# The query latents of a hybrid attention layer, projected beside the first norm, one tile ahead

## The chip, the cores and the metric

The kernel runs on one core of one Trainium2 chip. The metric is the device time of one execution in microseconds (us), as the median of several runs. A profiled execution of the same program gives the trace; its times count from the start of its span. In the text PE is TensorE (PEld its weight loads), DVE is VectorE, ACT is ScalarE, POOL is GpSimd, and SP is the engine that issues the DMAs here.

## The reference

One layer of a streaming encoder on x of 1024 frames by 1024 channels, all in float32. What matters here is the start:

```
h   = rms_norm(x, ln_mix_pre)
z   = h @ w_in                      # 1024 x 5824 columns
qa, ka, va, cq, ckv, k_rope, g_a, g_b = split(z)   # 1024,1024,1024,384,256,64,1024,1024
...                                 # differential attention from rope(qa), rope(ka), va
cq  = rms_norm(cq, q_a_norm)        # the query latents
qb  = cq @ w_uq                     # later: the second attention (latent, 8 heads)
...
merged = sigmoid(g_a) * y_a + sigmoid(g_b) * y_b
x   = x + rms_norm(merged @ w_o, ln_mix_post)
x   = x + rms_norm(SwiGLU(rms_norm(x, ln_ffn_pre)), ln_ffn_post)
```

Only cq's place in the program changes; nothing that is computed does.

## The kernel before, in words

Every float32 matrix product is made of three matmuls on two-part operands (a high and a low part, `mm3`, lines 266 to 269: high by high on L267, high by low on L268, low by high on L269). So each operand must first be split: ACT writes the high part, and DVE or POOL subtracts to get the low part (`split_sbuf`, lines L254 and L256, for loaded weights; `split_psum`, L260 and L261, for results in PSUM).

The start of the program (the prologue) works on tiles of 128 frames, from tile 7 down to tile 0. `norm_x` (L422 on) loads a tile of x, squares and sums it on ACT (L439), makes 1/rms with a small DVE step (L245) and a power on POOL (L247), scales it on DVE (L441), transposes it on PE in two groups of four (L447), and splits each group into hT, which all projections read. `da_proj` (L546) loads the weights of one head of the differential attention, splits them, and projects tile after tile with 24 matmuls of 384 columns each; then it applies the rotary tables (`rope`), which `rotary_tables` computes on DVE in the prologue. In the main program (L1335 on) head 0 of `da_proj` runs beside `norm_x`.

Then the eight heads of the differential attention follow. Beside the attention of each head (`interleave`) the PE is given filler work: the next head's projection and what the table `FILL` (L63) names: numbers are gate tiles (`gate_tile`, 48 matmuls of 512 columns each), "cq" and "ckv" are the latents (`latents`, L482). "cq" is done beside head 2: per tile of frames 24 matmuls of 384 columns, a square and sum on ACT (L500), 1/rms (L245, L247), a scaling on DVE (L502), three transposes on PE (L518) one tile later, a copy on ACT (L521) and a store. After the attention come the second attention, the merge (`mix_out`) and the feed-forward part, which the change doesn't touch in the source.

The program is written as one stream, from which a scheduler makes one fixed order per engine. Each engine takes its own instructions strictly in that order; an instruction waits at the head of its engine until the semaphores it names are reached. SBUF is dealt out by hand in zones (`Zone`), PSUM in banks (`Banks`). `cos_blk` and `sin_blk` are the rotary tables' two blocks.

## Time and profile before

| | |
|---|---|
| median of 3 runs | 2030.16 us (2027.11 to 2030.21) |
| profiled execution | 2029.12 us |
| its span, first to last instruction | 2027.1 us |
| PE busy in the span | 1968.2 us (97%) |
| DVE, ACT, POOL busy | 1162.7, 863.4, 537.7 us |
| PE waits in total, of that before its first instruction | 58.9 us, 11.8 us |
| granted PE clock, mean | 0.993 |

How to read it: PE is the engine that all others serve, so the time is PE's own work plus what it waits, plus what it loses while its clock is at the lower level. The total of the waits is the span less the busy time. The other engines are busy for little more than half of the span; what counts of them is only whether they deliver in time.

### The profile page before, as it was taken

How to read it: one execution, taken by the hardware profiler on the slowest of the kernel's cores; microseconds unless marked ns; L12 is line 12 of the kernel's file. 1: busy time of each engine (PE TensorE's matmuls, PEld its weight loads, DVE VectorE, ACT ScalarE, POOL GpSimd, SP SyncE). 2: the span in 40 equal slices, each digit the busy share in tenths (PEclk: the TensorE clock that was granted, in tenths of full speed). 3: DMA queues.
4: the chain of work that ended last, by engine and by line, in shares of the span. 5: the costliest groups of instructions: out<-in, count | busy, mean ns of one | idle time of the engine just before them, and what ended most of it. 6: DMA issues, size and time to landing. Idle time of an engine off the chain costs nothing. (4 is left out here: it accounts for less than half of the span.)

```text
span 2027.1 us, 28588 instructions
## 1 busy us (share of the span) xinstructions
PE 1968.2 (97%) x10400; PEld 1697.3 (84%) x10400; DVE 1162.7 (57%) x2464; ACT 863.4 (43%) x1912; POOL 537.7 (27%) x652
## 2 busy tenths in 40 slices
PE   6999999999999999999999998979999999999998
PEld 6898999989898988888978886757888888888886
DVE  7756757776775677786762355575344444343335
ACT  5435444554544446666663333343333323341102
POOL 2000010200000012222121212356554554452214
PEclk9999999999999999999999999989999999999999
DMA  5212111111212131450043533213222222262214
GB/s 169 69 47 81 44 57 51 56 49 43 77 33 77 35 111 53 132 174 29 32 149 100 168 125 107 91 63 94 76 90 84 73 94 73 102 231 83 83 32 145
DMA packets 148492, 176.49 MB, mean 87 GB/s; under 512 B 13536, under 2 KB 117376, under 8 KB 148352
## 3 DMA queue, kind: packets, MB, share of 16 engines
q1 hardware_dynamic: 148352, 174.68, 27.5%
q8 instruction: 81, 1.33, 0.3%
q14 instruction: 59, 0.48, 0.1%
HBM read 130.54 MB, written 44.11 MB: 86 GB/s over the span
## 5 line engine op out<-in xcount | busy, mean ns | idle before, releaser
L267 PE MATMUL PS<-AR 128*128 128x512 f32 (+3 forms) x2216 | 794.6, 361 | 4.7 <-ACT AR L254 2.0
L268 PE MATMUL PS<-AR 128*128 128x512 f32 (+3 forms) x2216 | 784.2, 355 | 3.7 <-POOL AR L256 3.7
L269 PE MATMUL PS<-AR 128*128 128x512 f32 (+3 forms) x2216 | 785.3, 356 | 1.7 <-POOL AR L256 1.7
L254 ACT CAST AR<-AFm 128x512 fp32r<-128x512 f32 (+4 forms) x514 | 301.3, 610 | 510.0 <-PE PS L1226 207.9
L267 PEld LDWEIGHTS PS<-AR 128*128 128x128 f32 x2216 | 417.2, 189 | 58.8 <-ACT AR L260 5.2
L268 PEld LDWEIGHTS PS<-AR 128*128 128x128 f32 x2216 | 418.7, 189 | 47.6 <-POOL AR L256 4.5
L269 PEld LDWEIGHTS PS<-AR 128*128 128x128 f32 x2216 | 417.4, 189 | 46.0 <-POOL AR L256 2.5
L256 POOL TENSOR_TENSOR AR<-AFm,AR 128x512 fp32r<-128x512 f32 (+4 forms) x203 | 310.0, 1533 | 459.8 <-ACT AR L254 408.6
L1226 PE MATMUL PS<-AR 128*128 128x512 f32 x1848 | 424.2, 391 | 5.4 <-POOL AR L256 3.7
L1226 PEld LDWEIGHTS PS<-AR 128*128 128x128 f32 x1848 | 348.0, 189 | 81.2 <-POOL AR L256 4.7
L256 DVE TENSOR_TENSOR AR<-AFm,AR 128x512 fp32r<-128x512 f32 (+5 forms) x311 | 212.7, 713 | 108.1 <-ACT AR L254 81.5
L260 ACT CAST AR<-PS 128x512 fp32r<-128x512 f32 (+3 forms) x320 | 135.2, 439 | 154.5 <-DVE AFm L388 70.6
L1235 DVE TENSOR_TENSOR AFm<-AFm,PS 128x512 f32<-128x512 f32 x110 | 75.3, 685 | 181.0 <-PE PS L1226 180.1
L261 DVE TENSOR_TENSOR AR<-PS,AR 128x512 fp32r<-128x512 f32 (+3 forms) x320 | 153.5, 497 | 40.1 <-ACT AR L260 38.1
L628 POOL CAST AR<-AR 128x128 fp32r<-128x128 f32 (+1 forms) x128 | 41.9, 327 | 455.4 <-PE PS L699 260.0
L658 ACT ACTIVATE AFm<-PS,nm 128x1024 f32<-128x1024 f32 (+3 forms) x192 | 142.7, 745 | 42.7 <-DVE nm L657 30.3
L657 DVE TENSOR_REDUCE nm<-PS 128x1 f32<-128x1024 f32 (+3 forms) x192 | 143.6, 752 | 3.3
L1298 DVE TENSOR_TENSOR AFm<-AFm,PS 128x512 f32<-128x512 f32 x80 | 54.4, 685 | 103.2 <-PE PS L269 103.2
L1190 DVE TENSOR_TENSOR AFm<-AFm 128x512 f32<-128x512 f32 x66 | 71.3, 1080 | 64.6 <-DMA s_aa<-AFm 27.6
L636 POOL MEMSET AR<- 128x256 f32 x64 | 21.2, 332 | 294.9 <-PE PS L269 244.8
L618 PE MATMUL PS<-idf,AFm 128*128 128x128 f32 x576 | 89.1, 275 | 2.5 <-ACT AR L260 0.6
L716 PE MATMUL PS<-AR 128*128 128x512 f32 (+5 forms) x384 | 87.1, 353 | 0.2 <-ACT AFm L658 0.2
(133 smaller groups left out, 1532.6 us busy)
## 6 DMA issues: line engine op xcount, KB each, us to landing
AFm<-in_w_in_dram SPq DMA_DIRECT2D x72, 192.0 KB
AFm<-in_w_ffn_gate_dram SPq DMA_DIRECT2D x22, 512.0 KB
AFm<-in_w_ffn_up_dram SPq DMA_DIRECT2D x22, 512.0 KB
s_aa<-AFm SPq DMA_DIRECT2D x44, 256.0 KB
AFm<-in_w_ffn_down_dram SPq DMA_DIRECT2D x22, 512.0 KB
AFm<-s_aa SPq DMA_DIRECT2D x22, 512.0 KB
AFm<-in_x_dram SPq DMA_DIRECT2D x16, 512.0 KB
AFm<-in_w_in_dram SPq DMA_DIRECT2D x32, 256.0 KB
```

What stands on the lines that cost most here:

```text
L254: nc.scalar.copy(h, src)
L256: e.tensor_tensor(out=l, in0=src, in1=f32v(h), op=ALU.subtract)
L260: nc.scalar.copy(h, src)
L261: nc.vector.tensor_tensor(out=l, in0=src, in1=f32v(h), op=ALU.subtract)
L267: nc.tensor.matmul(o, lhsT=sh, rhs=mh, start=first, stop=False)
L268: nc.tensor.matmul(o, lhsT=sh, rhs=ml, start=False, stop=False)
L269: nc.tensor.matmul(o, lhsT=sl, rhs=mh, start=False, stop=last)
L618: nc.tensor.transpose(tb.ap[:, q * P:(q + 1) * P], C[:, (g + q) * P:(g + q + 1) * P], idf)
L657: nc.vector.tensor_reduce(out=nm[:, m:m + 1], in_=src, axis=ax, op=ALU.max, negate=True)
L658: nc.scalar.activation(out=dst, in_=src, func=ACTF.Exp, bias=nm[:, m:m + 1], scale=1.0, accum_out=ss[:, m:m + 1])
L716: nc.tensor.matmul(sb.ap[:, c * 512:c * 512 + step], lhsT=qs.ap[:, m * 256 + v * P:m * 256 + v * P + P], rhs=kT[:, m, c * step:(c + 1) * s ...
L1226: nc.tensor.matmul(o, lhsT=v[:, ws, k], rhs=m, start=first and k == 0 and x == 0, stop=k == 3 and x == 2, skip_group_check=True)
```

## The change

The query latents cq leave the filler work beside head 2 and are projected in the prologue, tile by tile, right behind each tile's transposes. Their weights go to SBUF columns from 32768 on, which the attention uses later, so that the weights of `da_proj` can be loaded into their own zone while these are still in use. `norm_x` is cut in two: `scale(t)` (load, square, 1/rms, scaling) is now issued one tile ahead of the transposes, and it scales in place; the squares' unneeded output goes to `cos_blk`, and ln_mix_pre sits in `sin_blk`, so the rotary tables are written only behind the last scaling. `rotary_tables` starts with the third tile, as does `da_proj` of head 0. The gate tiles are dealt anew over the eight heads, 3, 2, 2, 0, 2, 2, 2, 3 (before 4, 2, 0, 0, 2, 2, 3, 3).

```diff
--- before.py
+++ after.py
@@ -60,7 +60,7 @@
 
 W_ENG = "dve"
 L_ENG = lambda nc: nc.vector
-FILL = ((0, 1, 2, 3), (4, 5), ("cq",), ("ckv",), (6, 7), (8, 9), (10, 11, 12), (13, 14, 15))
+FILL = ((0, 1, 2), (3, 4), (5, 6), ("ckv",), (7, 8), (9, 10), (11, 12), (13, 14, 15))
 PRE = 1
 DA_DEPTH = 1
 MLA_DEPTH = 2
@@ -426,20 +426,24 @@
             xts[t] = f_gen.alloc(D)
             nc.sync.dma_start(xts[t].ap, x2d[t * P:(t + 1) * P, :])
 
+        def scale(t):
+            ss = st("ss")
+            nc.scalar.activation(out=cos_blk.ap, in_=xts[t].ap, func=ACTF.Square, accum_out=ss)
+            r = rstd(ss, 1, D)
+            nc.vector.scalar_tensor_tensor(out=xts[t].ap, in0=xts[t].ap, scalar=r, in1=sin_blk.ap, op0=ALU.mult, op1=ALU.mult)
+
+
         load(NT - 1)
+        nc.sync.dma_start(sin_blk.ap, ln_mix_pre[0].partition_broadcast(P))
+        load(NT - 2)
+        scale(NT - 1)
         yield 0.0
-        wb = f_gen.alloc(D)
-        nc.sync.dma_start(wb.ap, ln_mix_pre[0].partition_broadcast(P))
         for t in reversed(range(NT)):
+            if t > 1:
+                load(t - 2)
             if t:
-                load(t - 1)
-            xt = xts.pop(t)
-            xs = f_gen.alloc(D)
-            ss = st("ss")
-            nc.scalar.activation(out=xs.ap, in_=xt.ap, func=ACTF.Square, accum_out=ss)
-            r = rstd(ss, 1, D)
-            nc.vector.scalar_tensor_tensor(out=xs.ap, in0=xt.ap, scalar=r, in1=wb.ap, op0=ALU.mult, op1=ALU.mult)
-            xt.free()
+                scale(t - 1)
+            xs = xts.pop(t)
             for g in range(2):
                 pb = ps_a.alloc()
                 for i in range(4):
@@ -451,15 +455,14 @@
                 pb.free()
             xs.free()
             yield 0.0
-        wb.free()
-
-
-    def load_win(lo, n, per):
+
+
+    def load_win(lo, n, per, zone=None):
 
         ws = []
         for k in range(0, NK, per):
             src = w_in[k * P:(k + per) * P, lo:lo + n].rearrange("(k p) c -> p k c", p=P)
-            ws.append(load_hl(src, f_raw, z_w, per * n, "p (k c) -> p k c", eng=W_ENG, k=per))
+            ws.append(load_hl(src, f_raw, zone or z_w, per * n, "p (k c) -> p k c", eng=W_ENG, k=per))
         return [(ws[k // per].h[:, k % per, :], ws[k // per].l[:, k % per, :]) for k in range(NK)], ws
 
     def gate_tile(j):
@@ -479,19 +482,20 @@
         for o in own:
             o.free()
 
-    def latents(which):
+    def latents(which, banks=ps_p, zone=None):
         if which == "cq":
             lo, n, nw, nrm, dst = 3072, 384, 384, q_a_norm, s_cq
         else:
             lo, n, nw, nrm, dst = 3456, 320, 256, kv_a_norm, s_ckv
-        w, own = load_win(lo, n, 1)
+        w, own = load_win(lo, n, 1, zone)
         wb = f_gen.alloc(nw)
         nc.sync.dma_start(wb.ap, nrm[0].partition_broadcast(P))
         nb = nw // P
         late = None
+        yield 0.0
         for t in reversed(range(NT)):
             sl = slice(t * P, (t + 1) * P)
-            pb = ps_p.alloc()
+            pb = banks.alloc()
             o = pb.ap[:, 0:n]
             for k in range(NK):
                 mm3(o, hT[:, k, 0, sl], hT[:, k, 1, sl], w[k][0], w[k][1], k == 0, k == NK - 1)
@@ -1335,18 +1339,21 @@
     all_slots = [[None] * 4 for _ in range(NH + 1)]
     nx, tab = norm_x(), rotary_tables()
     next(nx)
-    next(tab)
-    next(nx)
-    first = da_proj(0, all_slots[0], Banks(mp, 0, 6))
+    first, second = latents("cq", Banks(mp, 0, 6), Zone(mr, (32768, AR_COLS))), da_proj(0, all_slots[0], Banks(mp, 0, 6))
     next(first)
-    for _ in range(NT):
-        next(tab, None)
-        next(nx, None)
-        next(tab, None)
+    for t in range(NT):
+        next(nx)
+        next(first)
+        if t == 2:
+            next(second)
+        if t > 1:
+            next(tab, None)
+            next(tab, None)
+    drain(nx)
+    drain(first)
     drain(tab)
-    drain(nx)
     neg_lam, sub8 = lambda_column()
-    drain(first)
+    drain(second)
     M = Mla()
     hs = [{} for _ in range(NH + 1)]
 
```

The scheduler's order changes with it. On DVE, where the first tiles are scaled and split, the order before was (L441 scales a tile of x, L256 splits weights, L261 makes the low part of the transposed tile; L340 to L350 are the rotary tables):

```order
L441 SCALAR_TENSOR_TENSOR AFm<-AFm,rs_r 128x1024
L245 TENSOR_SCALAR rs_v<-ss 128x1
L341 TENSOR_SCALAR AFm<-AFm 128x256
L256 TENSOR_TENSOR AR<-AFm,AR 128x384
L441 SCALAR_TENSOR_TENSOR AFm<-AFm,rs_r 128x1024
L256 TENSOR_TENSOR AR<-AFm,AR 128x384
L261 TENSOR_TENSOR AR<-PS,AR 128x4x128 x2
L256 TENSOR_TENSOR AR<-AFm,AR 128x384 x2
L261 TENSOR_TENSOR AR<-PS,AR 128x4x128 x2
```

In the changed program the same place on DVE reads as follows (L433 scales a tile of x, L506 scales a tile of the latents):

```order
L433 SCALAR_TENSOR_TENSOR AFm<-AFm,rs_r 128x1024
L256 TENSOR_TENSOR AR<-AFm,AR 128x384 x8
L245 TENSOR_SCALAR rs_v<-ss 128x1
L261 TENSOR_TENSOR AR<-PS,AR 128x4x128
L433 SCALAR_TENSOR_TENSOR AFm<-AFm,rs_r 128x1024
L261 TENSOR_TENSOR AR<-PS,AR 128x4x128
L245 TENSOR_SCALAR rs_v<-ss 128x1
L506 SCALAR_TENSOR_TENSOR AFm<-PS,rs_r,AFm 128x384
L245 TENSOR_SCALAR rs_v<-ss 128x1
L433 SCALAR_TENSOR_TENSOR AFm<-AFm,rs_r 128x1024
L261 TENSOR_TENSOR AR<-PS,AR 128x4x128 x2
L256 TENSOR_TENSOR AR<-AFm,AR 128x384 x4
```

All eight weight splits now stand on DVE, and the two L261 of tile 6 stand behind the scaling of tile 7's latents (L506) and of the next tile of x but one (L433, tile 5).

On ACT in the same stretch of the changed program (L431 squares a tile of x, L504 squares a tile of latents, L525 copies transposed latents, L260 makes the high part of a transposed tile):

```order
L260 CAST AR<-PS 128x4x128
L504 ACTIVATE AFm,ss<-PS 128x384
L431 ACTIVATE AFm,ss<-AFm 128x1024
L260 CAST AR<-PS 128x4x128 x2
L254 CAST AR<-AFm 128x384 x8
L504 ACTIVATE AFm,ss<-PS 128x384
L525 COPY AFm<-PS 128x384
L431 ACTIVATE AFm,ss<-AFm 128x1024
L260 CAST AR<-PS 128x4x128 x2
```

A tile's high parts stand behind the squares of the latents of the tile before it, in every round.

On PE, the end of tile 6's latents and the begin of tile 5's in the changed program (L522 transposes latents, L451 transposes a tile of x):

```order
L268 MATMUL PS<-AR 128x384
L269 MATMUL PS<-AR 128x384
L522 MATMUL PS<-idf,AFm 128x128 x3
L451 MATMUL PS<-idf,AFm 128x128 x8
L267 MATMUL PS<-AR 128x384
L268 MATMUL PS<-AR 128x384
L269 MATMUL PS<-AR 128x384
```

Between the last matmul of one tile and the first of the next stand only 11 transposes.

## Rows read from the trace of the kernel before

**Rows 1.** The page's first part: busy time of each engine.
```profile
PE 1968.2 (97%) x10400; PEld 1697.3 (84%) x10400; DVE 1162.7 (57%) x2464; ACT 863.4 (43%) x1912; POOL 537.7 (27%) x652
```
**Rows 2.** PE's waits in the whole span: us in total, times, longest.
```profile
PE PS L447 <- DVE rs_v L245: 11.8, 1, 11.8
PE PS L1226 <- POOL AR L256: 3.7, 2, 2.5
...
PE PS L447 <- DVE AR L261: 2.9, 3, 2.3
...
PE PS L447 <- DVE AFm L441: 1.4, 2, 0.9
...
PE PS L518 <- DVE AFm L502: 0.5, 1, 0.5
```
**Rows 3.** Timeline of the first tile (start us, us, instruction, [idle before it]).
```profile
4.56 1.06 ACT L439 ACTIVATE AFm<-AFm 128x1024 f32<-128x1024 f32 x1 [2.55 <-DMA AFm<-in_x_dram]
...
8.80 0.15 DVE L245 TENSOR_SCALAR rs_v<-ss 128x1 f32<-128x1 f32 x1
...
9.10 0.59 POOL L247 TENSOR_TENSOR rs_r<-rs_v,mhalf 128x1 f32<-128x1 f32 x1 [7.51 <-DVE rs_v L245]
...
10.46 1.28 DVE L441 SCALAR_TENSOR_TENSOR AFm<-AFm,rs_r 128x1024 f32<-128x1024 f32 x1
...
11.79 1.97 PE L447 MATMUL PS<-idf,AFm 128*128 128x128 f32 x8 [11.79 <-DVE rs_v L245]
```
**Rows 4.** Timeline of the second tile and of the flow after it.
```profile
10.64 1.49 ACT L254 CAST AR<-AFm 128x384 fp32r<-128x384 f32 x3
...
11.91 0.55 DVE L256 TENSOR_TENSOR AR<-AFm,AR 128x384 fp32r<-128x384 f32 x1
...
12.85 5.16 POOL L256 TENSOR_TENSOR AR<-AFm,AR 128x384 fp32r<-128x384 f32 x4
12.91 2.01 DVE L441 SCALAR_TENSOR_TENSOR AFm<-AFm,rs_r 128x1024 f32<-128x1024 f32 x1 [0.45 <-POOL rs_r L247]
...
20.54 0.34 PE L268 MATMUL PS<-AR 128*128 128x384 f32 x1
...
20.72 0.33 PE L269 MATMUL PS<-AR 128*128 128x384 f32 x1
...
23.50 1.04 PE L447 MATMUL PS<-idf,AFm 128*128 128x128 f32 x8
```
**Rows 5.** Timeline of one tile of latents beside head 2, behind its last matmul.
```profile
253.52 0.50 ACT L500 ACTIVATE AFm<-PS 128x384 f32<-128x384 f32 x1
...
253.90 0.20 ACT L500 ACTIVATION_READ_ACCUMULATOR AFm<-PS 128x1 f32 x1
...
254.95 0.62 DVE L502 SCALAR_TENSOR_TENSOR AFm<-PS,rs_r,AFm 128x384 f32<-128x384 f32 x1 [0.66 <-POOL rs_r L247]
```
**Rows 6.** Groups by shape, 20 to 60 us; L521 from 250 to 305 us.
```profile
L261 DVE TENSOR_TENSOR AR<-PS,AR 128x512 fp32r<-128x512 f32 x13 | 8.6, 684 | 0.7 <-ACT AR L260 0.6
...
L260 ACT CAST AR<-PS 128x512 fp32r<-128x512 f32 x13 | 7.2, 588 | 9.7 <-PE PS L447 8.8 <-DVE AR L261 0.9
...
L521 ACT COPY AFm<-PS 128x384 f32<-128x384 f32 x8 | 3.8, 476 | 3.1 <-PE PS L518 3.1
```
**Rows 7.** PE's timeline around a wait in the merge.
```profile
1230.73 1.43 PE L267 MATMUL PS<-AR 128*128 128x512 f32 x5 [1.14 <-ACT AR L254]
1234.58 0.56 PE L268 MATMUL PS<-AR 128*128 128x512 f32 x1 [2.42 <-POOL AR L256]
...
1238.33 0.39 PE L269 MATMUL PS<-AR 128*128 128x512 f32 x1
```
**Rows 8.** Windows of 1 us; the last column is GB/s of DMA.
```profile
11.00:12.00 1.00, 0.21 (x1) 0.21 (x2) 1.00 (x4) 0.93 (x3) 0.12 (x1) 1.00 1.21 290
...
14.00:15.00 1.00, 0.59 (x2) 0.08 (x1) 1.00 (x2) 1.00 (x3) 1.00 (x1) 1.00 1.06 405
```

## The prediction

> **What bounds the kernel now.** I read the page's busy times first [rows 1]: PE works 1968.2 of 2027.1 us, no other engine more than 1162.7. So the time is PE's work plus what PE loses, and since the change neither adds nor removes a matmul, only the losses can move. The waits of PE [rows 2] say where they lie: 11.8 us before its first instruction, then 2.9 and 1.4 us at the transposes of the first tiles (L447). That is 16.1 us in the prologue. At the latents beside head 2 the largest entry is 0.5 us (L518): there they are well covered, so moving them away frees almost nothing. The prologue therefore decides.
>
> I count PE's losses in the prologue as time minus work at full rate. At full rate a matmul of 384 columns starts 0.175 us after the one before (20.54, 20.72) and eight transposes take 8 x 0.11 us (1.04 us with the last one's end) [rows 4].
>
> **Losses before.** By 23.50 us [rows 4] PE has done 16 transposes and 24 matmuls: 16 x 0.11 + 24 x 0.175 = 6.0 us of work, so 17.5 us are lost (the wait for the first tile, the first work at half rate, the wait of 2.3 us that is the longest of its row [rows 2]). Of the 2.9 + 1.4 us of waits, 2.0 us come after that. Sum: **19.5 us**.
>
> **Losses after: the first tile.** The square of x is ready as before: 4.56 + 1.06 us and 0.20 us to read the sum [rows 3, 5]. Then 1/rms, 0.85 us from the read's end to the start of the scaling where nothing stands in between (254.10 to 254.95 [rows 5]; here before it stood behind table work, from 5.8 to 10.46 us [rows 3]), the scaling 1.28 us [rows 3], so the transposes come at about 8.0 instead of 11.79 us, if ln_mix_pre has landed; at the worst they stay at 11.79. But this head start isn't what PE's next step waits for. The new DVE order has all eight weight splits (L256) ahead of the first low part of hT (L261), and PE's third matmul needs that. The first weight was cast at 10.64 us [rows 4]. The two table loads are now queued later, which I put at 1 us earlier (0 to 2). The weights are 1.57 MB: 5.4 us at 290 GB/s, 3.9 us at 405 GB/s [rows 8], the first being a stretch of these weights in runs of 512 bytes, the second of tiles in runs of 4096; the new runs of 1536 lie between, I take 4.5. So the last lands at about 9.6 + 7/8 x 4.5 = 13.5 us (12.0 to 15.3), is cast (0.5) and split (0.55) [rows 4] by 14.5 with the handovers, and L261 (0.68 [rows 6]) ends at 15.2. From there 22 matmuls: PE has stood idle, and in the trace it runs at half rate for 3.75 us after such a wait (1234.58 to 1238.33 [rows 7]), which is 11 of them; the other 11 take 1.9. The first tile's latents end at 20.9 us. Work by then is 0.9 + 4.2, the loss **15.8 us**.
>
> **The round.** Here is the cost. Say the latents of tile t end on PE at E. In the new order DVE must scale those latents (L506) and the tile of x two ahead (L433) before it makes the low part of the tile that PE needs next (L261), and ACT must square both before it makes the high part. This is a closed chain, and nothing of it can start before E:
> - square of the latents, read, 1/rms, scaling: 2.05 us from start to end (253.52 to 255.57 [rows 5]);
> - 1/rms of x behind it: 0.15 us less overlap and the power, together 0.85 us [rows 5];
> - scaling of x 1.28 us [rows 3], low part 0.68 us [rows 6];
> - handovers between engines, some 0.2 us in all.
>
> Sum 5.0 us. In that time PE has eight transposes and two matmuls, 1.2 us: it loses 3.8 us with tile 6. With tile 5 ACT has also the copy of transposed latents ahead of the square (0.48 us [rows 6]: 0.70 + 0.48 + 1.26 us on ACT is then the longer way, 0.4 us more) and PE three transposes more: 3.9 us. Before, each tile's low part waited only for its own transposes, and nothing of a projection's end stood ahead of it. From tile 4 on the weights of head 0 are there and its matmuls, 24 per tile, stand between in PE's order, 4.2 us that cover the rest of the round. What stays uncovered there I put at 1.0 us for each of the five tiles: the copy's 0.48 us, for which the second group of transposes waits (its PSUM bank), and a like amount at the low part; 0.4 (the 2.0 us of now over five tiles) to 1.6. So 3.8 + 3.9 + 5.0 = **12.7 us**.
>
> **The clock in the rounds.** The waits split in two (until the high part, until the low part), about 1.4 and 2.2 us, with two matmuls between. The nearest rows are waits of 1.14 and 2.42 us with five matmuls between, after which PE ran at half rate for 3.75 us [rows 7]. That loses 1.9 us per round, **3.8 us** for tiles 6 and 5. Bounds: nothing, or half rate to the round's end (4.2 us each).
>
> **POOL beside DVE.** In tile 6's round POOL splits four weights of head 0 while DVE scales x. In the trace that scaling took 2.01 instead of 1.28 us beside the same four (5.16 us together) [rows 3, 4]: **0.7 us**. [...]
>
> **What I cost at nothing.** The gate tiles dealt anew are the same matmuls, hidden or not by the same attention; the projection's place for its weights is free until the attention begins. The latents gone from head 2 give back their waits, **0.5 us** [rows 2] (at most 2). The scheduler also shuffles some splits in the feed-forward part, where PE waits 3.7 us for POOL now [rows 2]; I take 0, at worst 3 us.
>
> **Sum.** 15.8 + 12.7 + 3.8 + 0.7 = 33.0 us lost against 19.5, so 13.5 us more, less 0.5: 13 us. The profiled execution took 2029.1 us, which makes 2042.1; it lies 1.0 us under the median of the runs shown, so I forecast **2043 us**.
>
> **Rivals.**
> - *The clock stays up* through the rounds of tiles 6 and 5: 3.8 us less, 2039 us. For it: the two waits of a round are each short. Against it: the rows above. [...] No run here shows such a pair in a row of rounds. Chance 0.20.
> - *The clock stays down* from the first tile to the end of tile 5's round: 24 x 0.175 = 4.2 instead of 1.9 us lost in three rounds, 7 us more, 2050 us. For it: PE is busy for little more than half of a round. Chance 0.17.
> - *The head start wins* (not slower): the low parts come in time because the chain behind E is shorter than PE's own 1.2 us. Then the loss is the first tile's with the early weights, 14.5 us, plus the 2.0 us of now, 16.5 us, 3 us less than before; with the 0.5 us 2026.6 us. It decides at the point where L261 of the next tile needs nothing from the latents just ended. The order of DVE speaks against it, plainly; only a scheduler's order that I misread speaks for it. Chance 0.08.
> - The forecast itself: 0.55.
>
> **How the numbers follow.** The range runs from 2033 us (clock up, weights early, tiles 4 to 0 covered as now) to 2053 us (clock down, feed-forward 3 us worse). A measurement of this kernel can tell about 0.2%, 4 us, from no change. Faster than that: half of the head start's case, 0.04. Within it: the rest of that case and a little of the low end, 0.08. Slower: 0.88.
>
> **What would show it.** Right: in the first 45 us PE's waits at L269 for DVE's L261 of about 2 us each and at L267 for ACT's L260 of about 1.5 us, in two or three rounds about 9 to 11 us apart; transposes starting near 8 us; matmuls of 384 columns at 0.35 us apart behind the waits; no gain beside head 2. Wrong: if the third matmul of tile 6 starts within 2 us of the end of tile 7's latents, there is no round, and the time is near 2027. If the rounds are there but the time is much above 2053, the rotary tables, now written behind the last scaling, hold back head 0's projection, which I have at nothing because PE has the gate tiles' matmuls meanwhile.

## The result and the profile after

The changed kernel takes **2048.26 us** (median of 4 runs, 2046.03 to 2051.74) against 2029.70 us of the kernel before (4 runs, 2027.11 to 2030.21): a ratio of **1.0092, 95% interval 1.0081 to 1.0104**, so 18.6 us slower. The forecast was 2043 us, with a range of 2033 to 2053 us. The profiled execution took 2049.20 us, its span is 2047.1 us.

The page's first part, which answers to [rows 1]: PE has the same 10400 instructions. Of the 20.0 us that the span is longer, its busy time takes 10.4 us (matmuls at half rate count as busy: one of 384 columns with 0.52 us, against 0.33 to 0.34 at full rate) and its waits the rest.

```profile
PE 1978.6 (97%) x10400; PEld 1703.8 (83%) x10400; DVE 1155.8 (56%) x2464; ACT 864.0 (42%) x1914; POOL 531.9 (26%) x652
```

PE's waits in the whole span (us in total, times, longest), against [rows 2]:

```profile
...
PE PS L451 <- DVE AFm L433: 7.9, 1, 7.9
PE PS L269 <- DVE AR L261: 7.3, 7, 2.7
PE PS L267 <- ACT AR L254: 5.7, 3, 3.4
PE PS L267 <- ACT AR L260: 4.9, 8, 1.7
...
PE PS L268 <- DVE AR L256: 1.6, 1, 1.6
```

The wait before the first transposes fell from 11.8 to 7.9 us, as forecast. In its place stand two rows that the kernel before hardly had: the low part (L269 for L261) and the high part (L267 for L260) of a transposed tile. Two more, L267 for L254 (3.4 us at one time) and L268 for DVE's L256 (1.6 us), lie at 1813 us, in the down-projection, which the change does not touch. (The longest row of either trace, 13.1 us before and 11.7 us after, lies between 1260 and 1370 us, around the end of the merge, and is left out here.)

Where the 20 us came about is seen when the same matmul is looked up in both traces (start in us, worked out by counting matmuls from a fixed place):

| the same matmul | before | after | later by |
|---|---|---|---|
| last scores of the differential attention | 782.8 | 795.4 | 12.6 |
| first of the feed-forward part | 1341.9 | 1356.2 | 14.3 |
| a quarter into it | 1463.6 | 1475.3 | 11.7 |
| its end | 1778.1 | 1789.8 | 11.7 |
| last of the program | 2017.5 | 2037.5 | 20.0 |

So there are two places: the prologue (12.6 us, and the latents' freed place beside head 2 gives none of it back), and the down-projection (8.3 us), with small changes of +1.7 and -2.6 us between them.

**The prologue.** The round of tile 6, from the end of tile 7's latents on (start, us, instruction, idle time before it):

```profile
20.34 1.03 PE L451 MATMUL PS<-idf,AFm 128*128 128x128 f32 x8
20.54 0.49 ACT L504 ACTIVATE AFm<-PS 128x384 f32<-128x384 f32 x1 [7.26 <-PE PS L269]
...
21.02 1.05 ACT L431 ACTIVATE AFm<-AFm 128x1024 f32<-128x1024 f32 x1
...
21.97 0.62 DVE L506 SCALAR_TENSOR_TENSOR AFm<-PS,rs_r,AFm 128x384 f32<-128x384 f32 x1 [0.66 <-DMA AFm<-in_w_in_dram]
22.06 1.06 ACT L260 CAST AR<-PS 128x512 fp32r<-128x512 f32 x2
22.68 0.44 PE L267 MATMUL PS<-AR 128*128 128x384 f32 x1 [1.31 <-ACT AR L260]
23.31 1.29 DVE L433 SCALAR_TENSOR_TENSOR AFm<-AFm,rs_r 128x1024 f32<-128x1024 f32 x1 [0.66 <-POOL rs_r L247]
24.51 1.28 DVE L261 TENSOR_TENSOR AR<-PS,AR 128x512 fp32r<-128x512 f32 x2
25.25 0.44 PE L269 MATMUL PS<-AR 128*128 128x384 f32 x1 [1.95 <-DVE AR L261]
...
25.91 0.52 PE L269 MATMUL PS<-AR 128*128 128x384 f32 x1
26.23 0.52 PE L267 MATMUL PS<-AR 128*128 128x384 f32 x1
...
29.35 0.34 PE L268 MATMUL PS<-AR 128*128 128x384 f32 x1
...
33.47 0.44 PE L267 MATMUL PS<-AR 128*128 128x384 f32 x1 [0.87 <-ACT AR L260]
...
36.79 0.69 PE L269 MATMUL PS<-AR 128*128 128x384 f32 x1 [2.69 <-DVE AR L261]
```

This is the closed chain of the prediction, link by link: square of the latents, their scaling (L506), 1/rms and scaling of x (L433, 23.31), low part (L261, 24.51), and only then PE's third matmul at 25.25, 4.9 us after the latents' end. ACT likewise squares latents and x before it makes the high part (22.06). Behind the two waits the matmuls are 0.32 us apart (25.91 to 26.23) until 29.11 us, then 0.17 again. The same pair of waits comes again in tile 5's round, before 33.47 and 36.79 us (0.87 and 2.69 us), and there the matmuls are 0.32 us apart until 42.7 us. In windows of 10 us (length, busy time and instructions of PE, PEld, DVE, ACT and POOL, then PEclk, DMA share, GB/s) the granted clock is the third value from the end, and PE's busy time the second of the row:

```profile
20.00:30.00 10.00, 6.74 (x31) 6.16 (x31) 7.49 (x12) 5.88 (x14) 6.06 (x6) 0.83 0.65 152
30.00:40.00 10.00, 6.16 (x29) 5.33 (x28) 8.98 (x24) 4.00 (x9) 1.15 (x2) 0.80 0.60 164
40.00:50.00 10.00, 9.12 (x46) 8.29 (x45) 6.29 (x16) 2.96 (x7) 1.25 (x2) 0.86 0.35 95
```

**The down-projection.** Lines from the timelines of PE, POOL, SP and ACT around the place where PE runs dry (L1254 multiplies gate by up, L1256 stores the product s_aa, L285 loads the down-projection's operands):

```profile
1788.35 4.75 POOL L256 TENSOR_TENSOR AR<-AFm,AR 128x1024 fp32r<-128x1024 f32 x2 [3.49 <-ACT AR L254]
1793.06 2.55 POOL L1254 TENSOR_TENSOR AFm<-AFm 128x512 f32<-128x512 f32 x2
1795.64 0.33 SPq L1256 DMA_DIRECT2D s_aa<-AFm  x1
1796.76 5.00 SPq L285 DMA_DIRECT2D AFm<-s_aa  x4
1803.23 7.12 POOL L256 TENSOR_TENSOR AR<-AFm,AR 128x1024 fp32r<-128x1024 f32 x3 [7.62 <-ACT AR L254]
1805.67 2.69 SPq L285 DMA_DIRECT2D AFm<-in_w_ffn_down_dram  x2
1810.38 0.33 SPq L285 DMA_DIRECT2D AFm<-s_aa  x1
1814.23 1.04 ACT L254 CAST AR<-AFm 128x1024 fp32r<-128x1024 f32 x1 [1.06 <-DMA AFm<-s_aa]
1816.76 0.50 PE L267 MATMUL PS<-AR 128*128 128x512 f32 x1 [3.43 <-ACT AR L254]
1818.85 0.79 PE L268 MATMUL PS<-AR 128*128 128x512 f32 x1 [1.59 <-DVE AR L256]
...
1820.30 0.63 PE L268 MATMUL PS<-AR 128*128 128x512 f32 x1
1820.72 0.63 PE L269 MATMUL PS<-AR 128*128 128x512 f32 x1
```

POOL makes two low parts (4.75 us) before the last two products; the last store goes out at 1795.64 us, and four loads of s_aa behind it. Followed back from PE's wait, the trace leads to POOL's next three low parts, made one after the other (7.12 us): only at their end, 1810.38 us, can the next load of s_aa go out, its cast comes at 1814.23 us, and the cast that PE needs stands behind that one on ACT. PE stands still at 1813 and 1817 us. Behind that its matmuls of 512 columns are 0.42 us apart instead of 0.23 until about 1824 us. Wait and half rate together are the 8.3 us.

A late last store is not what sets this apart from the kernel before, where POOL also makes low parts between the last products:

```profile
1777.78 0.42 SPq L285 DMA_DIRECT2D AFm<-s_aa  x1
...
1786.64 0.32 SPq L1252 DMA_DIRECT2D s_aa<-AFm  x1
...
1787.53 0.40 SPq L285 DMA_DIRECT2D AFm<-s_aa  x1
```

There the last store goes out 8.5 us behind the start of the feed-forward part's last matmul (1778.1 us), in the changed kernel 5.8 us behind it (1789.8 us). But in the kernel before six of the 22 loads of s_aa have gone out ahead of the last store (the sixth at 1777.78 us), in the changed kernel only four. What put the loads in another order had to be found by experiment.

### The profile page after: what moved, and what is told of

The parts are those of the page before. It is cut to its first block, busy times and chain, and to the rows that moved or that the text cites. A ratio compares the mean times of both kernels' runs of the same rounds, so it can differ in the third digit from the quotient of the medians.

```text
span 2047.1 us, 28554 instructions
## 1 busy us (share of the span) xinstructions
PE 1978.6 (97%) x10400; PEld 1703.8 (83%) x10400; DVE 1155.8 (56%) x2464; ACT 864.0 (42%) x1914; POOL 531.9 (26%) x652
## 5 line engine op out<-in xcount | busy, mean ns | idle before, releaser
L267 PE MATMUL PS<-AR 128*128 128x512 f32 (+3 forms) x2216 | 797.1, 363 | 14.9 <-ACT AR L254 5.7
L269 PE MATMUL PS<-AR 128*128 128x512 f32 (+3 forms) x2216 | 788.3, 357 | 9.2 <-DVE AR L261 7.3
L268 PE MATMUL PS<-AR 128*128 128x512 f32 (+3 forms) x2216 | 787.6, 357 | 5.4 <-POOL AR L256 3.6
L254 ACT CAST AR<-AFm 128x512 fp32r<-128x512 f32 (+6 forms) x514 | 300.8, 610 | 514.4 <-PE PS L1230 206.3
L267 PEld LDWEIGHTS PS<-AR 128*128 128x128 f32 x2216 | 419.8, 190 | 71.1 <-ACT AR L260 10.4
L269 PEld LDWEIGHTS PS<-AR 128*128 128x128 f32 x2216 | 419.5, 190 | 55.9 <-DVE AR L261 10.1
L268 PEld LDWEIGHTS PS<-AR 128*128 128x128 f32 x2216 | 421.0, 190 | 49.7 <-POOL AR L256 4.5
L256 POOL TENSOR_TENSOR AR<-AFm,AR 128x512 fp32r<-128x512 f32 (+4 forms) x203 | 307.4, 1522 | 457.1 <-ACT AR L254 410.3
L256 DVE TENSOR_TENSOR AR<-AFm,AR 128x512 fp32r<-128x512 f32 (+5 forms) x311 | 208.4, 701 | 104.4 <-ACT AR L254 94.9
L260 ACT CAST AR<-PS 128x512 fp32r<-128x512 f32 (+2 forms) x320 | 135.2, 440 | 139.8 <-DVE AFm L388 71.4
L261 DVE TENSOR_TENSOR AR<-PS,AR 128x512 fp32r<-128x512 f32 (+2 forms) x320 | 153.1, 497 | 40.0 <-ACT AR L260 38.3
```

The source lines that it names most:

```text
L254: nc.scalar.copy(h, src)
L256: e.tensor_tensor(out=l, in0=src, in1=f32v(h), op=ALU.subtract)
L260: nc.scalar.copy(h, src)
L261: nc.vector.tensor_tensor(out=l, in0=src, in1=f32v(h), op=ALU.subtract)
L267: nc.tensor.matmul(o, lhsT=sh, rhs=mh, start=first, stop=False)
L268: nc.tensor.matmul(o, lhsT=sh, rhs=ml, start=False, stop=False)
```

## The experiments

Each kernel was run in a group beside the kernel before, on one chip per group; ratios are to it, with the 95% interval. From group to group the median of before moved between 2028.9 and 2030.7 us, so runs of different groups are compared by their ratios or by the differences to their own before.

### The rooms of the feed-forward part

The rooms (columns of SBUF) are dealt while the program is written: of the free places that fit, `Zone` takes the one that was let go longest ago; `Banks` does the same for the banks of PSUM. So a change in the prologue leaves another history of releases behind, and temporaries and loads far later get other rooms. The scheduler sees other dependencies, and orders them differently. Two kernels test it. The first is the changed kernel with the history of before put in just ahead of the merge, for the columns of the float32 room (`mf`) and for the PSUM banks (`mp`), which are always exchanged together here:

```diff
+    mf.when[:] = np.repeat([6, 9, 12, 13, 2, 8, 11, 14, 4, 10, 3, 5, 7, 1, 0],
+                           [16] * 13 + [2, 2])
+    mp.when[:] = [4, 5, 6, 7, 2, 3, 0, 1]
     mix_out(X, prefetch)
```

> The changed kernel, with the history of releases of the f32 room (which room was let go when) and of the PSUM banks set, just ahead of the merge, to what it is there in the kernel before. So the temporaries of the feed-forward part and the first loads of the down-projection get the rooms of the kernel before; the prologue stays. Theory of the rooms: the wait of 5.8 us at 1813 us and the half clock behind it (together 8.3 us) come from loads that wait for a room which a later step still uses, and go; the 2.6 us that the changed kernel gains between the start of the feed-forward part and its first quarter go too. 2048.3 - 8.3 + 2.6 = 2042.6 us (2040 to 2045), no wait of PE over 1 us in the down-projection. Rival, the time of day: the operands come late because all engines stand otherwise to one another after the prologue, whatever the rooms: 2048 us, the wait still there.

Measured: 2042.28 us, ratio 1.0064 (1.0052 to 1.0077), against 1.0092 with the kernel's own rooms. PE has no wait at all between 1785 and 1830 us. By the same matmuls the trace's feed-forward part takes 437.6 us and its down-projection 239.4 us; in the kernel before it is 436.2 and 239.4 us, in the changed kernel 433.6 and 247.6 us.

The second is the reverse: the kernel before, no latents moved, with the history of the changed kernel.

```diff
+    mf.when[:] = np.repeat([11, 5, 8, 10, 1, 6, 2, 13, 12, 7, 4, 3, 9, 0],
+                           [16] * 13 + [4])
+    mp.when[:] = [6, 7, 4, 5, 2, 3, 0, 1]
     mix_out(X, prefetch)
```

> The reverse: the kernel before, untouched but for the history of releases just ahead of the merge, which is set to that of the changed kernel. No latents move. Theory of the rooms: it becomes slower by 8.3 - 2.6 = 5.7 us, 2035.4 us (2033 to 2038), with the changed kernel's wait of PE at the first block of the down-projection, some 5 to 6 us in all, and half clock behind it. Rival, the time of day: 2030 us and no such wait.

Measured: 2033.04 us, ratio 1.0021 (1.0012 to 1.0031), 4.2 us slower. Its waits of PE from 1790 to 1830 us:

```profile
PE PS L267 <- ACT AR L254: 6.3, 1, 6.3
PE PS L268 <- DVE AR L256: 1.3, 1, 1.3
```

The theory of the rooms holds in both directions, the time of day falls: with the histories exchanged and nothing else, the wait in the down-projection comes and goes, and so does the small gain in the first quarter of the feed-forward part (432.1 us in this trace, its down-projection 250.5 us). The size of the reverse, 4.2 us, is a little under the 5.7 us expected. Whether the columns or the PSUM banks decide was not tested apart.

Which rooms are good is no property of the prologue. With the transposes moved (next section) and rooms of its own, the feed-forward part came out differently a third time:

> The changed kernel with the transposes of a tile ahead of the latents of the tile before it, and nothing else: the history of releases is left to what the program makes of it, so the feed-forward part gets rooms of its own, neither those of before nor those of the changed kernel. With the rooms of before it took 2032.6 us. Theory of the rooms: they decide the feed-forward part and the down-projection within some 9 us, by chance: 2028 to 2037 us, with or without a wait of PE at the first blocks of the down-projection, and the prologue is the same to 0.5 us. Rival, the rooms matter in the changed kernel only because of its prologue's times: 2032 to 2033 us, and no wait there.

Measured: 2034.32 us, ratio 1.0021 (1.0012 to 1.0030), the same ratio as with the rooms of before, but made up otherwise: by the same matmuls its feed-forward part takes 2.2 us less than that of its twin with the rooms of before, and its down-projection 4.8 us more, with PE waiting for ACT's L254 (1.2 us) and DVE's L256 (1.3 us) from 1802 us on. The waits speak for the theory; the time alone does not tell it from the rival.

Last, who holds the rooms. The first six low parts of s_aa go to DVE:

```diff
-            aa.append(load_hl(s_aa[f * P:(f + 1) * P, :], f_dn, z_dn, S))
+            aa.append(load_hl(s_aa[f * P:(f + 1) * P, :], f_dn, z_dn, S, eng="dve" if f < 6 else "pool"))
```

> The changed kernel, its own rooms everywhere, with one thing else: the low parts of the first six row blocks of the gated products, which the down-projection loads first, are made by DVE instead of POOL. Theory of the rooms, and of who holds them: the loads behind the first block wait for a room in the f32 zone, and a room comes free only when POOL, at 2.4 us a split, has made its low part; DVE needs 1.23 us. Then the two waits of PE at 1813 us (3.4 and 1.6 us) and the half clock behind them go, 8 us (5 to 9) less than the changed kernel: 2040 to 2043 us, with the prologue as it is. Rival, the rooms are late because of the order on SP alone (the stores of the products and the loads share its queue): within 2 us of 2048 us, the waits still there.

Measured: 2041.92 us, ratio 1.0061 (1.0047 to 1.0075). Of the waits at 1813 us one of 0.5 us is left. Timelines of DVE, POOL and SP:

```profile
1785.35 2.35 DVE L256 TENSOR_TENSOR AR<-AFm,AR 128x1024 fp32r<-128x1024 f32 x2
1791.05 1.30 POOL L1254 TENSOR_TENSOR AFm<-AFm 128x512 f32<-128x512 f32 x1 [0.46 <-DVE AFm L1239]
1792.37 0.33 SPq L1256 DMA_DIRECT2D s_aa<-AFm  x1
1793.45 4.20 SPq L285 DMA_DIRECT2D AFm<-s_aa  x4
```

Two splits take 2.35 us on DVE where POOL took 4.75; the products no longer stand behind them, and the loads go out at 1793.45 instead of 1796.76 us. With that the changed kernel is as fast as with the rooms of before (1.0061 and 1.0064), and its down-projection takes 240.1 us. The edit also lets the scheduler order this stretch anew, so it does not say how much is due to the faster split and how much to the order.

### The closed round

These kernels have the rooms of before in the feed-forward part, so they are compared with 1.0064. First, the transposes of the next tile are issued ahead of the latents of this one:

```diff
+    next(nx)
     for t in range(NT):
-        next(nx)
+        next(nx, None)
         next(first)
```

> The changed kernel with the rooms of the kernel before in the feed-forward part, and with one step of the norm drawn before the loop, so that the transposes and splits of a tile are issued ahead of the latents of the tile before it. Nothing of a round is then behind the end of those latents. Theory of the closed round: the losses at the low parts and high parts of tiles 6, 5 and 4 and the half clock behind them go, 11 to 13 us of the 12.6 us that the prologue loses, against 2042.6 us with the rooms alone: 2030 to 2032 us; PE waits under 1 us between 25 and 60 us. Rival, the first tile: the loss sits in the weights that come late and all eight splits on DVE, which stay: at most 3 us better, 2040 us or more. Rival, the tables: they are written behind the last scaling and hold back head 0's projection: then the wait only moves to 60 to 110 us, and the time stays near 2042 us.

Measured: 2032.57 us, ratio 1.0021 (1.0012 to 1.0030): 9.7 us of the 13.4 us are gone with two lines. Two of its windows:

```profile
20.00:30.00 10.00, 9.96 (x64) 9.46 (x64) 6.66 (x11) 8.42 (x21) 4.86 (x5) 1.00 0.72 163
30.00:40.00 10.00, 6.80 (x34) 6.15 (x33) 8.55 (x23) 4.52 (x10) 3.53 (x5) 0.83 0.67 188
```

From 20 to 30 us PE is now busy for 9.96 us instead of 6.74. Counted as in the prediction (time minus work at full rate, until 120 us), the prologue loses 24.4 us instead of 34.2 us with the rooms alone. It was expected that PE waits under 1 us between 25 and 60 us; that failed at one new wait, the only one between 25 and 40 us:

```profile
PE PS L522 <- DVE AR L261: 3.1, 1, 3.1
```

The transposes of the latents (L522) need a PSUM bank that L261 of the tile ahead must empty first, and DVE makes this L261 late. Its timeline, L506 of 0.62 us left out (the last row is POOL's):

```profile
26.82 3.37 DVE L256 TENSOR_TENSOR AR<-AFm,AR 128x384 fp32r<-128x384 f32 x4
...
32.75 2.01 DVE L433 SCALAR_TENSOR_TENSOR AFm<-AFm,rs_r 128x1024 f32<-128x1024 f32 x1 [0.45 <-POOL rs_r L247]
34.68 1.27 DVE L261 TENSOR_TENSOR AR<-PS,AR 128x512 fp32r<-128x512 f32 x2
...
32.68 0.99 POOL L256 TENSOR_TENSOR AR<-AFm,AR 128x384 fp32r<-128x384 f32 x1
```

Four splits of head 0's weights, the latents' scaling and the scaling of x stand in front of it. The rival of the first tile (at most 3 us better) and that of the tables (the wait only moves to 60 to 110 us, where 0.6 us are left) fall.

Then each half of the change alone. The norm one tile ahead, with cq back beside head 2:

```diff
-FILL = ((0, 1, 2), (3, 4), (5, 6), ("ckv",), (7, 8), (9, 10), (11, 12), (13, 14, 15))
+FILL = ((0, 1, 2, 3), (4, 5), ("cq",), ("ckv",), (6, 7), (8, 9), (10, 11, 12), (13, 14, 15))
...
-    next(first)
+    next(second)
     for t in range(NT):
         next(nx)
-        next(first)
-        if t == 2:
-            next(second)
```

> One part of the change alone: the norm one tile ahead, scaled in place, with the tables written behind it, but the query latents back beside head 2 and the gate tiles dealt as in the kernel before; rooms of the feed-forward part as before. Theory of the closed round: without the latents no tile's low part stands behind the end of a projection; the transposes begin near 8 instead of 11.8 us, and what the late tables cost at head 0's projection is some 3 us: 2028 to 2034 us. Rival, the norm ahead itself is what costs (the scaling of the next tile in front of the low part of this one, the tables late): 8 us or more of the 12.6 stay, 2038 us or more.

Measured: 2031.97 us, ratio 1.0015 (1.0007 to 1.0024). PE's waits in the first 70 us:

```profile
PE PS L267 <- ACT AR L260: 3.1, 1, 3.1
PE PS L451 <- DVE AR L261: 3.0, 1, 3.0
PE PS L267 <- DVE AR L261: 2.5, 1, 2.5
```

There is no round; each of these waits comes once. The head start buys nothing, since PE now waits for the first weights and splits behind the first transposes (the first two rows, before 13.1 and 17.1 us), but the norm ahead is not what costs most: 3.1 us over before, of the 13.4.

The other half, the latents in the prologue with each tile of x scaled in its own step. In this kernel the last tile of x is squared and scaled after the rotary tables have been written, so its unneeded squares overwrite the cosines and it is scaled by sines instead of ln_mix_pre; the instructions and their sizes are the same.

```diff
-            if t:
-                scale(t - 1)
+            scale(t)
             xs = xts.pop(t)
```

> The other part of the change alone: the latents in the prologue as in the changed kernel, but each tile of x squared and scaled in its own step, right ahead of its transposes, not one tile ahead (in place as before in the changed kernel); rooms of the feed-forward part as before. Theory of the closed round: the latents behind the transposes make the round, and without the head start the square and the scaling of x come into it whole: 4 us (2 to 8) slower than 2042.3 us, 2046 us (2044 to 2050). Rival, scaling one tile ahead is what costs, because it puts the next tile's work in front of this tile's low part: faster than 2042 us by 3 us or more.

Measured: 2051.12 us, ratio 1.0103 (1.0087 to 1.0118): 21.0 us over before, 7.6 us more than with the norm ahead. The direction is that of the closed round; the size is at the upper end of what was expected. Of PE's waits in the first 70 us one row says why:

```profile
PE PS L449 <- DVE AFm L433: 16.7, 3, 7.8
```

After the first 7.8 us PE waits two more times, 8.9 us together, for the scaled tile itself. So the latents in the prologue make the round, and the norm ahead takes part of it away. The two halves do not simply add: 3.1 and 21.0 us alone, 13.4 us together.

One link of the chain alone: the scaling of the next tile issued behind the splits of this one.

```diff
-            if t:
-                scale(t - 1)
             xs = xts.pop(t)
...
             xs.free()
+            if t:
+                scale(t - 1)
             yield 0.0
```

> The changed kernel with the rooms of the kernel before in the feed-forward part, and with the scaling of the next tile of x issued behind the splits of the tile at hand instead of ahead of them. On DVE the 1/rms and the scaling of x (1.29 us and what leads to it, some 2 us together) then no longer stand between the scaling of the latents and the low part; the latents' own square, 1/rms and scaling still do. Theory of the closed round: the wait at the low part shrinks by about 2 us in the rounds of tiles 5 and 4, and some half clock with it; against 2042.3 us with the rooms alone 4 us (2 to 6) less: 2038 us (2036 to 2040). Rival, the latents' chain alone sets the round (the scaling of x is hidden): 2042 us. Rival, the scaling of x is the whole round: 10 us less, 2032 us, as when the transposes go ahead.

Measured: 2040.19 us, ratio 1.0047 (1.0034 to 1.0059), 10.1 us over before instead of 13.4: 3.3 us of gain, within what was expected. The two intervals touch (1.0034 to 1.0059 here, 1.0052 to 1.0077 with the rooms alone), so the time alone hardly tells this from no gain; the traces do, with 29.6 us lost until 120 us here and 34.2 us there. PE's waits from 28 to 43 us:

```profile
PE PS L269 <- DVE AR L261: 1.3, 1, 1.3
```

The window of 30 to 40 us:

```profile
30.00:40.00 10.00, 8.14 (x52) 7.14 (x51) 9.02 (x26) 5.67 (x14) 1.74 (x3) 1.00 0.60 164
```

With the rooms alone the same stretch has 2.7 us for L261 and 0.9 us for L260, and PEclk 0.74 in that window. Tile 6's round stays as it was (waits of 1.3 and 1.9 us), so this link is one of several; by the traces neither rival holds.

What the prediction costed at nothing, the gate tiles dealt anew, taken back:

```diff
-FILL = ((0, 1, 2), (3, 4), (5, 6), ("ckv",), (7, 8), (9, 10), (11, 12), (13, 14, 15))
+FILL = ((0, 1, 2, 3), (4, 5), (), ("ckv",), (6, 7), (8, 9), (10, 11, 12), (13, 14, 15))
```

> The changed kernel with the rooms of the kernel before in the feed-forward part, and with the gate tiles dealt as before (4, 2, 0, 0, 2, 2, 3, 3, head 2 with no filler but the next head's projection). Theory, the gate tiles are hidden either way, as in the prediction: 2042 us (2040 to 2044), within 0.1 per cent of the rooms alone. Rival, the dealing costs or gives something in the differential attention: head 2 without filler waits for its own vector work, 3 us slower or more, 2045 us; or the new dealing itself costs, and the old one is 3 us faster, 2039 us.

Measured: 2042.31 us, ratio 1.0063 (1.0050 to 1.0075), the same as with the new dealing. The gate tiles are hidden either way.

### Putting it together

> What the runs so far point to, put together: transposes of a tile ahead of the latents of the tile before it; the transposes of the latents two tiles behind instead of one, so that the 3.3 us at 31.1 us, where PE waits for the scaling of the latents, go with the half clock behind them; the changed kernel's history of rooms from the merge on, which lets the feed-forward part start 3 to 4 us better; and the low parts of the first six blocks on DVE. Theory: against the kernel before, the prologue 3 us better (the 1.7 us that the first of these still loses, less 3.3 and 1.5), the feed-forward part 3 to 4 us better, the down-projection as before: 2029 - 6 = 2023 us (2021 to 2026), faster than both. Rival, the feed-forward part's gain is given back at the down-projection, as in every run with those rooms so far: 2031 us. Rival, the latents' transposes only wait at another place: 2028 us.

> The same without the set history: rooms as the program's own history makes them, so a feed-forward part and down-projection of its own. Theory of the rooms: the prologue is the same as in the run beside it to 0.5 us, and the rest differs by the rooms alone, by up to 6 us: 2023 to 2029 us. Rival, with the first six low parts on DVE the rooms no longer matter: within 1.5 us of the run beside it.

Both have the transposes of a tile ahead and the six low parts on DVE; the first also has the history of the changed kernel, with the numbers shown above. New in both is the edit to the latents' transposes:

```diff
-            if late is not None:
-                late()
+            if len(lates) > (which == "cq"):
+                lates.pop(0)()
...
+            lates.append(late)
```

Measured: 2028.06 us, ratio 0.9993 (0.9984 to 1.0001), and 2029.37 us, ratio 0.9995 (0.9986 to 1.0003). Both are about 1% faster than the changed kernel and not to be told from the kernel before; the 6 us better that was expected did not come. By the same matmuls, the prologue of the first run, expected 3 us better, loses as much as before (22.4 against 22.5 us until 120 us); the feed-forward part gains 2.2 us and the down-projection gives back 0.7. The rival about the latents' transposes was right, and the expectation had named the wrong releaser: not the latents' scaling but the bank that L261 empties. In the first run PE's waits from 0 to 70 us now read

```profile
PE PS L451 <- DVE AR L261: 2.0, 1, 2.0
```

and the wait has mostly gone from the latents' transposes (1.4 us for L261 are left) to those of x, which need such a bank too. Between the two runs the rival holds as well: they lie 1.3 us apart, within its 1.5 us and within the noise. By the same matmuls they agree to 0.3 us at the end of the differential attention and differ by 1.4 us at the end of the feed-forward part. The last run asks for the weights of head 0 one tile later:

```diff
-        if t == 2:
+        if t == 3:
             next(second)
```

> The run ahead_all with the weights of head 0 asked for one tile later. There PE still lost 1.2 and 2.2 us at 31 to 33 us, because DVE made four low parts of those weights (3.4 us beside POOL's) in front of the latents' scaling and the next low parts. Theory of the closed round, in its wider form (what stands on DVE in front of a tile's low part is what PE waits for, as long as PE has no other work): those losses shrink to 1 us or so together, with the 1 to 2 us of half clock behind them: 3 us (2 to 4) less than 2028.1 us, 2025 us. Rival, the splits only come in front of another tile's low part: 2027 to 2029 us.

Measured: 2028.84 us, ratio 0.9993 (0.9983 to 1.0002), nothing gained; the rival holds. PE still waits there, in the trace's row

```profile
PE PS L522 <- DVE AR L261: 3.3, 3, 2.8
```

DVE is busy 8.98 of the 10 us from 30 to 40 us in this run: table work, splits and scalings of x lie in one stretch there, so taking one thing from in front of a low part puts another in its place. No version beat the kernel before measurably.

## Why the prediction was right, and where it was not

The sign and the range held, and so did the mechanism, the closed round. Point by point, with losses counted as in the prediction (time minus work at full rate):

| step | forecast | measured in the trace of after |
|---|---|---|
| first transposes | near 8.0 us | 7.93 |
| first low part ends; third matmul | 15.2 us | 14.15; 14.21 |
| end of tile 7's latents; loss until then | 20.9; 15.8 us | 20.3; 15.3 us |
| round of tile 6, waits | 3.8 us | 3.7 us |
| round of tile 5, waits | 3.9 us | 4.5 us |
| half rate behind these two | 3.8 us | 1.7 + 2.9 = 4.6 us |
| tiles 4 to 0 | 5.0 us | 5.9 us (43 to 95 us) |
| POOL beside the scaling of x | 0.7 us | 0: L433 took 1.29 us |
| prologue, more than before | 13.5 us | 12.6 us (35.1 less 22.5, each until 120 us) |
| beside head 2 | -0.5 us | 0 |
| feed-forward part and what lies ahead of it | 0, at worst 3 us | +1.7 - 2.6 + 8.3 = +7.4 us |

**The first tile** went as worked out; the low part came 1 us earlier than the weights' rate had let me think, and half of that was lost again because PE's matmuls stayed 0.32 us apart for longer (14.69 to 18.85 us). **The round** has the price that the sum gave, 5.0 us forecast from the latents' end to the third matmul and 4.9 measured; putting the transposes ahead gave back 9.7 us of time, which shows it by experiment (the other 3.7 us of the 13.4 stayed, the new wait among them). **POOL** did not disturb the scaling: its first split of head 0's weights began at 24.02 us, 0.7 us after L433 had begun. The row was right, its place wrong (in the traces in which both were looked at, the scaling is lengthened only where POOL's split began first, 2.01 against 1.28 to 1.29 us): with the transposes ahead, POOL's split began at 32.68 us and L433 at 32.75, and this one took 2.01 us, as in [rows 4].

**The two totals** were both too low: 33.0 us forecast and 35.1 measured after, 19.5 and 22.5 before. So part of the good fit of their difference, 13.5 against 12.6, is luck. Of the baseline, 27 and not 24 matmuls had started by 23.50 us, so 17.0 us were lost there instead of 17.5; but behind it PE lost 5.5 us until 120 us, not the 2.0 us of its waits, as losses that the trace lists as no wait were left out.

**The step that failed** is the sentence "The scheduler also shuffles some splits in the feed-forward part ... I take 0, at worst 3 us". It measured 8.3 us in the down-projection, 7.4 us with what lies around it, and is the whole of the miss: 13 us forecast, 12.6 + 7.4 = 20.0 us in the traces. I had seen that the order differed there and priced it by the waits of the kernel before, which had none in the down-projection; the runs with rooms exchanged showed that a place without a wait can get one of 6 us when its loads are dealt other rooms. The time stayed in the range although this term lay beyond its worst case of 3 us: the upper end had room for 7 us of clock that were not needed. The lower end, 2033 us, does not follow from the three things named for it: 3.8, 1.3 and 3.0 us off 2043 make 2035 us.

**The rivals.** *The clock stays up* fell: PE's matmuls were 0.32 us apart behind the two waits, in tile 6's round (1.31 and 1.95 us, with two matmuls between them) as in tile 5's (0.87 and 2.69 us), and PEclk 0.83 and 0.80 from 20 to 30 and from 30 to 40 us. That a pair of waits as short as these leaves the clock up was the author's assumption; neither round shows it. *The clock stays down* fell too, in tile 5's round narrowly: the matmuls were back at 0.17 us in tile 6's round from 29.35 us on, in tile 5's only from 42.97 us on, shortly before its end at 43.50. That the time came near this rival's 2050 us is a coincidence: another 7 us came from the feed-forward part. *The head start wins* fell in the changed kernel at the third matmul of tile 6, 4.9 us behind the latents' end, not within 2. The *rotary tables* held nothing back: from 60 to 110 us no wait is longer than 0.4 us.

What stays open: why these rooms and not others lead the scheduler to issue four instead of six loads of s_aa ahead of the last store. It was shown that the release histories decide whether the wait is there, and that low parts on DVE take it away; the chain through POOL's three low parts is read from one trace, and the single room or bank on which it hangs was not looked for.

## What to carry to other kernels

When a projection is moved right behind the transposes that feed it, look at what its result queues on the engines that must deliver the next tile: if its normalisation stands there ahead of the next splits, the two form a closed loop, and PE waits once per tile until other work stands between; here one tile of transposes ahead broke it and gave back 9.7 of 13.4 us. When places in SBUF are dealt by release history, an edit at the start of a program can cost several us at its end: compare the order of loads and stores everywhere, not only around the edit, and exchange the histories to tell such an effect from the edit's own. Where loads wait for buffers, try the split that frees a buffer on the faster of the two engines; here DVE took 2.35 us for two splits of 128x1024 where POOL took 4.75, and all but 0.5 us of a wait of 5 us went away.

## What was not expected of the hardware

A pair of short waits was followed by the lower clock level, as one longer wait of 3.1 us was. In tile 6's round of the changed kernel it was 1.31 and 1.95 us with two matmuls between, and the matmuls went to 0.32 us apart 0.7 us after the second wait had ended (25.25 to 25.91 us). The delay differed from round to round: in tile 5's (0.87 and 2.69 us) the first matmul behind the second wait, at 36.79 us, was slow already (0.69 us, against 0.44 at 25.25 us). With a single wait of 1.3 us for the low part, and two of 0.3 us besides from 28 to 43 us, PEclk was 1.00 (30 to 40 us, scaling behind the splits); with a single one of 3.1 us between 25 and 40 us it was 0.83 (30 to 40 us, transposes ahead). At the start of the span the column is no guide: it says 1.00 from 10 to 20 us of the changed kernel, where the matmuls are 0.32 us apart from 14.69 to 18.85 us.

The scaling of x was lengthened where a split of POOL had begun before it, and not where one began behind it. It took 1.29 us where POOL's split began 0.7 us behind it (24.02 us, changed kernel), and 2.01 us where POOL's had begun 0.07 us before it (32.68 us, transposes ahead). Four more cases read the same: 2.01 us beside a split that had begun 0.06 us before it (12.85 us, kernel before, [rows 4]) or 0.07 us before it (31.36 us, weights later), and 1.28 us beside one that began 0.65 us behind it (25.06 us, transposes ahead) or 0.31 us behind it (24.27 us, weights later). At 32.75 us of the run with the transposes ahead, POOL's split lasted 0.99 us, 0.92 us of it beside L433, and L433 became 0.73 us longer than at 24.41 us (2.01 against 1.28). Why the order of the two beginnings makes this difference, no run shows.
